# One order of the text for all engines, from the first load of x to the norm of k

## The chip, the cores and the metric

The kernel runs on one core of one Trainium2 chip. The metric is the device time of one execution in microseconds (us); lower is better. Times of the kernel before: 1184.32, 1184.76 and 1186.61 us in three runs, median 1184.76.

## What is computed

One layer of a hybrid decoder on x of 1024 positions by 1024 features in float32. Only the beginning matters here:

```
h = rmsnorm(x) * mix_norm
[q | k | v | u | s | gate_a | gate_b] = h @ w_in
q = rmsnorm(q per head) ; k = rmsnorm(k per head)      # 8 q heads, 2 kv heads of 64
```

After it come sliding-window attention, a spatial gating unit over chunks of 128 positions, a gated merge through three more products, and a gated MLP with a causal convolution of width 3. The output is (1, 1024, 1024) float32.

## The kernel before, in words

Every product is made in three matmuls: each operand is split into a high part, rounded to the matmul's float32r type, and a low part, the rest, and high·high, high·low and low·high are added up in PSUM (`mm3`, L91, the matmuls of L93, L94 and L95). A high part is a copy on ScalarE (`copy_hi`, L88 and L89), a low part a subtraction on VectorE or GpSimd. So each operand costs work on ACT, on DVE or POOL, and on PE.

The stage in question multiplies x with the k and v columns of w_in. The contraction of 1024 is cut into eight chunks k = 0 to 7. One array, xw, holds for each chunk the 128 rows of the norm's gain, of the k and v weights (256 columns) and of x (1024 positions), 1281 numbers a row, 640.5 KB a chunk. What follows happens per chunk, L227 to L254:

- `xload` (L203) brings the chunk from HBM over SP's queue (L206 and L207 for chunk 0, in two parts; L209 for the rest). Chunks 0 to 2 have the tile xf for themselves; chunks 3 to 7 share three buffers of the tag xr, so chunk 6 goes where chunk 3 was, and chunk 7 where chunk 4 was, and each waits until every reader of the old one is done. Five chunks are loaded ahead (L221); chunk k + 5 is asked for at the end of the pass for chunk k (L243).
- L229 copies the high part of the weights (wkv) on ACT, L230 makes the low part on DVE. L233 and L234 do the same with x, times the gain, in two halves of 512 positions (three pieces for chunk 0).
- L239 makes the 24 matmuls of the chunk, eight groups of positions by three, into the PSUM tiles pkv.
- `xsquare(k - 1)` (L211) squares the chunk before on ACT (L215 for chunk 0, L218 for the rest) and adds it to a running sum on DVE (L219).
- At k = 2 the text loads the two halves of the q weights (wq; L99 through `rload`), ident and cp (L247, L248); at k = 4 the first u weights (wu, L99), sink and ali (L251, L252).
- At k = 5 `rsplit` (L188) makes the high part of wq's first half on ACT and its low part on POOL (L193). After chunk 7 come the square of chunk 7, the second half of wq, and the split of the u weights: high on ACT, low on DVE (L256 to L259).

Then PE sums the squares over the partitions with ones as moving operand (tile ssq, L321), makes the first two q blocks (`q_proj`, L263), and the norm of k and the transposes follow, with the lines to L419 in an order written out by hand.

Two things set the order on an engine. Inside a `tc.manual_schedule()` the engines keep the order of the text; `build` (L35) holds one for PE over the whole kernel. Where an engine is in none, the framework's scheduler chooses from its own model of the times. Before the change, a manual order of all engines held from L317 to L420, and again from L1970 to the end. From L121 to L316, and from L421 to L1969, ACT, DVE, POOL and SP were in the scheduler's hands.

The body is long; the program prints the part that the diff touches.

Of the kernel before, what the change touches and what calls it, by code (L numbers as in the profile page):

```python
# [34 lines left out]
def build(tc, a):  # L35
    nc = tc.nc
    ctx = ExitStack()
    with ctx, tc.manual_schedule(engines={mybir.EngineType.PE}):
        body(ctx, tc, nc, a)


def body(ctx, tc, nc, a):
# [37 lines left out]
    def PH(s):  # L80
        if psum.get("H") is None:
            return PS(s)[:, 0:512]
        return psum["H"].tile([128, 512], F, tag="H", name=nm(s))
# [119 lines left out]
    def xload(k):  # L203
        xr[k] = x_first[:, k, :] if k < 3 else pa.tile([128, 1281], F, tag="xr", name=nm("xr"), bufs=3)
        if k == 0:
            nc.sync.dma_start(xr[k][:, 0:513], a["xw"][k, :, 0:513])  # L206
            nc.sync.dma_start(xr[k][:, 513:1281], a["xw"][k, :, 513:1281])  # L207
        else:
            nc.sync.dma_start(xr[k], a["xw"][k])  # L209

    def xsquare(k):  # L211
        for c in (L, H):
# [5 lines left out]
            nc.scalar.activation(sq, xs, AF.Square)  # L218
            nc.vector.tensor_tensor(sqsum[:, c], sqsum[:, c], sq, op=ALU.add)  # L219

    for k in range(X_AHEAD):  # L221
        xload(k)
    warm = PH("warm")
# [90 lines left out]
    kss3 = kss.rearrange("p (s g) -> p s g", g=2)  # L314
    krs3 = krs.rearrange("p (s g) -> p s g", g=2)

    man = tc.manual_schedule()  # L317
    man.__enter__()
    p_ssq = PH("ssq")
    for s in range(8):  # L320
        nc.tensor.matmul(p_ssq[:, 2 * s:2 * s + 2], sqsum[:, s * 128:(s + 1) * 128], ones,  # L321
# [323 lines left out]
    man = tc.manual_schedule()  # L645
# [1400 lines left out]
```

## Time and profile before

| | |
|---|---|
| time, median of three runs | 1184.76 us |
| time of the profiled execution | 1185.26 us |
| its span in the profile | 1183.5 us |
| granted TensorE clock over the span, mean | 0.998 |
| instructions | 15928 |
| matmuls recorded in the span | 5842 |
| PE idle in the first 31.41 us | 3.0 us |
| PE idle from 50 to 200 us | 3.1 us |

A row of the timeline has the start and the length in us, the engine, the line, the operation, output <- input with sizes and count, and in brackets how long the engine stood idle before it and what ended that. SPq is the queue on which SP issues transfers; the length there is that of the issue and not of the transfer. A row of the table of stretches has the stretch, its length, then for PE, PEld (weight loads), DVE, ACT and POOL the busy time and the number of instructions, then the granted clock, the share of the DMA engines and GB/s. In the view of DMA issues the last number is the time from issue to landing.

### The profile page before, as it was taken

Reading aid. Unit: us, or ns where it says so; the run is one execution under the profiler, and the core shown is the slowest. Engines: PE = TensorE matmul, PEld = TensorE weight load, DVE = VectorE, ACT = ScalarE, POOL = GpSimd, SP = SyncE. Lnnn points to the kernel's source line nnn. Section 1 sums busy time; section 2 is a strip of 40 time slices with the busy share of each in tenths; the row PEclk is TensorE's granted clock in tenths of the full one; section 3 lists DMA queues with packets and bytes.
Section 4 is the critical chain, followed back from the end, with each engine's and each line's share of the span. In section 5 each row is a group of like instructions: output and inputs, shape, how many; then the busy total and the mean of one; then the engine's idle time right before and its main releaser. Section 6 shows DMA issues by size and latency. Waiting matters only on the chain.

```text
span 1183.5 us, 15928 instructions
## 1 busy us (share of the span) xinstructions
PE 1170.3 (99%) x5842; PEld 990.4 (84%) x5842; DVE 874.5 (74%) x1037; ACT 566.5 (48%) x878; POOL 631.8 (53%) x435
## 2 busy tenths in 40 slices
PE   8999999999999999999999999999999999999998
PEld 8989989988888878888878888888888888888887
DVE  7798975743536776678788788877888797875674
ACT  8555667644336653335444443444444445425331
POOL 2467685488884764444867677776767541000000
PEclk9999999999999999999999999999999999999999
DMA  7110136157556654454545445455555268975471
GB/s 272 37 55 19 54 130 228 56 168 239 161 160 204 233 193 154 146 176 132 138 129 169 118 149 152 142 141 134 166 137 160 72 219 287 365 232 196 155 231 67
DMA packets 80942, 188.66 MB, mean 159 GB/s; under 512 B 9184, under 2 KB 16864, under 8 KB 80736
## 3 DMA queue, kind: packets, MB, share of 16 engines
q1 hardware_dynamic: 73008, 167.58, 40.7%
q0 software_dynamic: 7456, 15.73, 8.0%
q10 hardware_dynamic: 400, 4.33, 1.1%
q8 instruction: 46, 0.75, 0.3%
q14 instruction: 32, 0.26, 0.1%
HBM read 146.97 MB, written 49.02 MB: 166 GB/s over the span
## 4 chain that ended last, share of the span: by engine, by line
PE 82%; DVE 4%; POOL 3%; ACT 2%; issue 2%; DMA 1%; DVEq 0%; POOLq 0%; SPq 0%; ACTq 0%
PE pz L1060 50%; PE pd L1855 10%; PE pdy L1855 8%; PE px L95 2%; PE px L93 2%; PE px L94 2%; PE pu L95 1%; PE pu L93 1%; PE pu L94 1%; PE pv L517 1%; PE pq L93 1%; PE pq L95 1%; PE pq L94 1%; DVE xa L621 1%; DMA lq<-wup 0%
## 5 line engine op out<-in xcount | busy, mean ns | idle before, releaser
L1060 PE MATMUL pz<-T,qh 128*128 128x512 f32 x472 | 145.6, 390 | 0.0
L1060 PE MATMUL pz<-B,ph 128*128 128x512 f32 x352 | 109.7, 393 | 0.7 <-ACT x L1695 0.7
L1060 PEld LDWEIGHTS pz<-T,qh 128*128 128x128 f32 x472 | 88.4, 188 | 18.6 <-ACT u L885 0.3
L1019 POOL TENSOR_TENSOR pl<-lp,ph 128x1024 fp32r<-128x1024 f32 x30 | 73.2, 2439 | 52.9 <-ACT ph L89 52.9
L1060 PE MATMUL pz<-T,ql 128*128 128x512 f32 x236 | 91.8, 389 | 0.0
L1019 POOL TENSOR_TENSOR ql<-lq,qh 128x1024 fp32r<-128x1024 f32 x30 | 76.8, 2559 | 9.1 <-ACT qh L89 9.1
L1060 PEld LDWEIGHTS pz<-B,ph 128*128 128x128 f32 x352 | 65.1, 188 | 16.7 <-ACT x L1695 3.8
L1078 DVE TENSOR_TENSOR pz<-pz,rstd_b 128x1024 f32<-128x1024 f32 x60 | 73.9, 1232 | 4.6 <-ACT rstd_b L143 2.5
L1060 PE MATMUL pz<-T,s3h 128*128 128x512 f32 x232 | 71.4, 389 | 0.0
L1060 PE MATMUL pz<-y,wjh 128*128 128x512 f32 x224 | 69.5, 391 | 0.6 <-POOL y L1233 0.3
L1060 PE MATMUL pz<-B,pl 128*128 128x512 f32 x176 | 68.6, 390 | 0.0
L1855 PE MATMUL pd<-bh,ah 128*128 128x512 f32 x176 | 68.5, 389 | 0.0
L1855 PE MATMUL pd<-bl,ah 128*128 128x512 f32 x176 | 68.5, 389 | 0.0
L1855 PE MATMUL pd<-bh,al 128*128 128x512 f32 x176 | 68.5, 389 | 0.0
L1060 PE MATMUL pz<-T,AX 128*128 128x512 f32 x264 | 63.4, 389 | 0.0
L1060 PE MATMUL pz<-B,AX 128*128 128x512 f32 x264 | 63.4, 389 | 0.0
L1019 POOL TENSOR_TENSOR s3l<-lq,s3h 128x512 fp32r<-128x512 f32 x20 | 26.0, 1298 | 62.3 <-ACT s3h L89 62.3
L1060 PEld LDWEIGHTS pz<-T,AX 128*128 128x128 f32 x264 | 49.5, 188 | 10.3
L1060 PEld LDWEIGHTS pz<-B,AX 128*128 128x128 f32 x264 | 49.6, 188 | 10.3
L89 ACT ACTIVATE AX<-lr 128x1024 fp32r<-128x1024 f32 x22 | 23.4, 1063 | 70.9 <-POOL lr L621 70.9
L621 DVE TENSOR_TENSOR pz<-pz,u 128x512 f32<-128x512 f32 x37 | 25.9, 700 | 42.5 <-ACT u L1072 36.2
L1550 DVE SCALAR_TENSOR_TENSOR tg<-pz,cp,tg 128x1023 f32<-128x1023 f32 (+1 forms) x44 | 56.2, 1278 | 0.8
(359 smaller groups left out, 3597.6 us busy)
## 6 DMA issues: line engine op xcount, KB each, us to landing
lp<-wup SPq DMA_DIRECT2D x22, 512.0 KB, 3.8
lq<-wup SPq DMA_DIRECT2D x22, 512.0 KB, 4.2
ra<-wdown SPq DMA_DIRECT2D x44, 256.0 KB, 4.9
b<-T SPq DMA_DIRECT2D x44, 256.0 KB, 3.5
lq<-wup POOLq DMA_DIRECT2D x42, 256.0 KB, 5.3
B<-tv SPq DMA_DIRECT2D x33, 256.0 KB, 2.0
T<-tt SPq DMA_DIRECT2D x33, 256.0 KB, 2.1
b<-B SPq DMA_DIRECT2D x33, 256.0 KB, 3.0
```

The lines of the kernel that those rows point to most:

```text
L89: return nc.scalar.activation(dst, src, AF.Copy, scale=scale)
L93: nc.tensor.matmul(out, wh, mh, start=first, stop=False, **kw)
L94: nc.tensor.matmul(out, wh, ml, start=False, stop=False, **kw)
L95: nc.tensor.matmul(out, wl, mh, start=False, stop=last, **kw)
L517: nc.tensor.matmul(o, vhl[:, kb, g, :], w[:, 2 * g:2 * g + 2, :], start=i == 0 and g == 0, stop=i == len(ops) - 1, skip_group_check=True)
L621: eng.tensor_tensor(out, x, y, op=op)
L1019: nc.gpsimd.tensor_tensor(l, r, h.bitcast(F), op=ALU.subtract)
L1060: nc.tensor.matmul(o, p[:, k, :], m, start=not more and k == 0 and j == 0, stop=k == nk - 1 and j == 2, skip_group_check=True)
L1078: nc.vector.tensor_tensor(z, z, rstd_b, op=ALU.mult)
L1550: nc.vector.scalar_tensor_tensor(t[:, j:], p[:, 0:1024 - j], cw[:, ci, 2 - j:3 - j], t[:, j:], op0=ALU.mult, op1=ALU.add)
L1855: nc.tensor.matmul(o[d], p[:, k - k0, m], q[:, k - k0, :], start=new and k == 0 and j == 0, stop=k == HK - 1 and j == 2, skip_group_check= ...
```

## The change

The manual order of all engines, which began before the sums of squares (L317), begins before the first load of x (L221). No instruction is added or removed, no size changes, and PE had the order of the text in both.

```
@@ -218,6 +218,8 @@
             nc.scalar.activation(sq, xs, AF.Square)
             nc.vector.tensor_tensor(sqsum[:, c], sqsum[:, c], sq, op=ALU.add)
 
+    man = tc.manual_schedule()
+    man.__enter__()
     for k in range(X_AHEAD):
         xload(k)
     warm = PH("warm")
@@ -314,8 +316,6 @@
     kss3 = kss.rearrange("p (s g) -> p s g", g=2)
     krs3 = krs.rearrange("p (s g) -> p s g", g=2)
 
-    man = tc.manual_schedule()
-    man.__enter__()
     p_ssq = PH("ssq")
     for s in range(8):
```

In the text's order SP issues: chunk 0 in two parts, chunks 1, 2, 3, 4, 5, 6 and 7, the two halves of wq, ident, cp, wu, sink, ali. ACT takes for each chunk the weights' copy, the copies of x, and the squares of the chunk before; after those of chunk 4 the copy of wq's first half, then chunk 6.

More of the change, by code (lines that the diff above doesn't have):

```diff
@@ L219, in xsquare @@
             nc.vector.tensor_tensor(sqsum[:, c], sqsum[:, c], sq, op=ALU.add)
+    man = tc.manual_schedule()
+    man.__enter__()
     for k in range(X_AHEAD):
@@ L315, in body @@
     krs3 = krs.rearrange("p (s g) -> p s g", g=2)
-    man = tc.manual_schedule()
-    man.__enter__()
     p_ssq = PH("ssq")
```

## The prediction

> **What bounds the kernel now.** I read the page's shares first, then the chain that ended last, then a table of stretches, and only then, engine by engine in order of time, the stretch that the diff touches.
>
> ```profile
> PE 1170.3 (99%) x5842; PEld 990.4 (84%) x5842; DVE 874.5 (74%) x1037; ACT 566.5 (48%) x878; POOL 631.8 (53%) x435
> ...
> PE 82%; DVE 4%; POOL 3%; ACT 2%; issue 2%; DMA 1%; DVEq 0%; POOLq 0%; SPq 0%; ACTq 0%
> ```
>
> PE is busy for 99% of the span and holds 82% of the chain. So a microsecond by which PE falls behind early stays in the time, unless a later PE gap takes it up. The next rows (stretch, its length, then busy time and count of PE, PEld, DVE, ACT, POOL, then the granted clock) cut the edited stage out.
>
> ```profile
> 6.30:8.10 1.80, 1.75 (x8) 1.13 (x8) 0.95 (x3) 1.08 (x3) 0.00 (x0) 1.00 0.91 335
> 8.10:11.51 3.41, 3.41 (x16) 3.41 (x17) 2.95 (x6) 3.41 (x8) 0.00 (x0) 0.51 0.99 400
> 11.51:31.41 19.90, 19.90 (x171) 19.90 (x170) 19.90 (x32) 18.85 (x34) 4.88 (x2) 1.00 0.65 233
> 31.41:50.00 18.59, 17.62 (x151) 17.25 (x150) 11.24 (x30) 6.86 (x14) 6.90 (x5) 1.00 0.17 59
> 50.00:200.00 150.00, 146.90 (x1067) 135.93 (x1067) 121.29 (x251) 96.14 (x278) 101.53 (x107) 1.00 0.25 89
> ```
>
> PE multiplies k and v from about 6 to 31.4 us, after 8.10 without a gap. From 8.10 to 11.51 it runs at half clock (0.51). DVE is full as well and ACT nearly. Whoever delays the x copies on ACT by more than PE's small lead delays PE.
>
> ```profile
> 6.30 0.38 PE L93 MATMUL pkv<-wkv,x 128*128 128x256 f32 x1 [1.89 <-ACT x L89]
> ...
> 31.05 0.28 PE L93 MATMUL pkv<-wkv,x 128*128 128x256 f32 x1
> ...
> 31.41 1.84 PE L321 MATMUL ssq<-ones,rstd_b 128*128 128x2 f32 x16
> ```
>
> Three matmuls lie between 31.05 and 31.41, so one costs 0.12 us (I use 0.118), and a block of 24 (block k works on chunk k of the contraction, 0 to 7) costs 2.83. Counting two blocks back from 31.41, block 6 began at 25.75 and its third matmul, the first to need DVE's low part, was due at 26.0. That is the time to beat.
>
> **The change, part by part.** Nothing is computed that was not computed before; four queues get another order. PE had its text order already. SP is the queue that moves most.
>
> ```profile
> 0.81 0.38 SPq L209 DMA_DIRECT2D xr<-xw  x1
> 1.24 0.42 SPq L206 DMA_DIRECT2D xf<-xw  x1
> 1.72 0.43 SPq L207 DMA_DIRECT2D xf<-xw  x1
> 2.19 0.91 SPq L209 DMA_DIRECT2D xf<-xw  x2
> 3.15 0.93 SPq L209 DMA_DIRECT2D xr<-xw  x2
> 4.12 1.44 SPq L99 DMA_DIRECT2D wq<-wq  x2
> ...
> 18.13 0.33 SPq L209 DMA_DIRECT2D xr<-xw  x1
> 18.50 0.51 SPq L251 DMA_DIRECT2D sink_b<-sink  x1
> 20.70 0.33 SPq L209 DMA_DIRECT2D xr<-xw  x1
> 21.13 0.38 SPq L252 DMA_DIRECT2D ali<-ali  x1
> ```
>
> The scheduler issued one xr tile (x3) first, then both parts of x0, x1, x2, x4, x5; then it pulled both wq loads to 4.12, ahead of x6 (18.13) and x7 (20.70), which must wait for a free slot among the three xr buffers. In the text, x6 and x7 stand at k=1 and k=2, and wq, ident, cp, wu, sink and ali stand behind them. So SP will wait at x6 until x3's slot is free, at x7 until x4's, and wq leaves only after x7.
>
> *At the front, a gain.* Landing is issue plus the last figure of these rows, each from the view of DMA issues in a narrow window: x3 (issued 0.81), the first and second part of x0 (1.24, 1.72), x1 (2.19), x7 (20.70), ali (21.13).
>
> ```profile
> xr<-xw SPq DMA_DIRECT2D x1, 640.5 KB, 4.0
> xf<-xw SPq DMA_DIRECT2D x1, 256.5 KB, 4.2
> xf<-xw SPq DMA_DIRECT2D x1, 384.0 KB, 5.3
> xf<-xw SPq DMA_DIRECT2D x1, 640.5 KB, 6.8
> xr<-xw SPq DMA_DIRECT2D x1, 640.5 KB, 3.9
> ali<-ali SPq DMA_DIRECT2D x1, 512.0 KB, 4.8
> ```
>
> They landed at 4.8, 5.4, 7.0, 9.0, 24.6 and 25.9: after the first, about 1.6 to 2 us for each 640.5 KB. Without x3 ahead of it x0 starts some 1.6 us earlier (first part about 3.9) and x1 lands where the second full 640.5 KB landed, at 7.0. PE thus starts at about 4.7 instead of 6.30, and the half clock of 8.10 to 11.51, which follows PE's wait of 1.89, may be gone too. I count neither: block 6 will wait for ACT, whatever PE has gained before.
>
> *ACT's pace.* Block by block ACT makes one wkv copy, two x copies, two squares of the block before.
>
> ```profile
> 15.47 0.40 ACT L89 ACTIVATE wkv<-xr 128x256 fp32r<-128x256 f32 x1
> ...
> 18.04 0.40 ACT L89 ACTIVATE wkv<-xr 128x256 fp32r<-128x256 f32 x1
> 18.35 1.33 ACT L89 ACTIVATE x<-xr 128x512 fp32r<-128x512 f32 x2
> 19.58 1.09 ACT L218 ACTIVATE sq<-xr 128x512 f32<-128x512 f32 x2
> 20.62 1.05 ACT L89 ACTIVATE wq<-wq 128x1024 fp32r<-128x1024 f32 x1
> 21.57 1.09 ACT L218 ACTIVATE sq<-xr 128x512 f32<-128x512 f32 x2
> 22.61 0.40 ACT L89 ACTIVATE wkv<-xr 128x256 fp32r<-128x256 f32 x1
> ```
>
> From 15.47 to 18.04 is 2.57 per block. Blocks 1 to 5 from 7.0 end at 7.0 + 5 × 2.57 = 19.85, with the square of x4 last. That square frees x7's slot: before, it ended at 20.67 and SP issued x7 at 20.70. So x7 leaves at 19.85 (and x6, one block earlier, at 17.3, landing 21.2).
>
> *The added wait.* At k=5 the text puts the split of wq's first half behind that square. Before, wq had long landed and ACT took the copy at 20.62, while x6 was still on its way. Now wq stands right behind x7. The nearest row is ali, also 512 KB and also next behind x7: it landed 25.93 − 20.70 = 5.23 after x7's issue. So wq lands at 25.1 and ACT stands still for 5.2 us. Behind the copy on ACT lie block 6's wkv and x copies, then block 7's; DVE's low parts wait for them, and PE for both. Bounds: wq can come with x7 itself, 3.9 + 0.4 behind its issue (0.9 earlier), or share its time with the second wq half behind it (1.3 later, what 512 KB took between x7 and ali). The start of ACT's blocks can move by −0.6 (x0's copies done sooner than x1 is counted) to +0.8 (the square as late as before). I take the ali row, as the same size in the same place.
>
> Then: copy of wq until 25.1 + 0.95 = 26.05 (20.62 to 21.57), wkv 0.31, first x copy 0.71 to 27.1: PE begins block 6. DVE's low part takes 0.75:
>
> ```profile
> 14.83 0.75 DVE L234 SCALAR_TENSOR_TENSOR x<-xr,x 128x512 fp32r<-128x512 f32 x1
> ...
> 18.35 1.28 DVE L219 TENSOR_TENSOR rstd_b<-rstd_b,sq 128x512 f32<-128x512 f32 x2
> 19.55 0.42 DVE L230 TENSOR_TENSOR wkv<-xr,wkv 128x256 fp32r<-128x256 f32 x1
> ```
>
> So the third matmul runs at 27.85 instead of 26.0: **+1.85**. DVE needs about 2.86 per block (two sums 1.20, wkv 0.33, two low parts 1.33), so block 7's first low part is there at 27.85 + 2.86 = 30.7, when PE gets to it; nothing is added.
>
> *The clock behind the gap.* PE's blocks 1 to 5 follow x1: its first low part is ready at 7.0 + 0.31 + 0.71 + 0.75 = 8.75, and five blocks end at 22.7. From there to 27.1 PE stands 4.4 us. The trace has the half clock after a wait of 1.89; I expect it here as well. A stretch of 3.41 us holds 16 matmuls (the row of 8.10) instead of 3.41 / 0.118 = 29; 13 × 0.118 = **+1.5**. Bounds: 0, if the clock stays, and 3.0, if two stretches follow. The Trainium skill, "TensorE: Matmul & The Clock Gate", section "HAM oscillation — how this bites in real kernels", speaks against the change in the same place: PE gaps above some 3.4 us bring the half clock, at about 1.67 us each; by it the sum would be an estimated 3.5. The trace is stricter than that threshold, since 1.89 us went before a half-clock stretch here.
>
> *What is hidden.* ident, cp, wu, sink and ali now follow wq. From x7's landing (23.75) they and wq are some 2,200 KB, at 512 KB in 1.3 us about 5.6 us: all landed near 29.4, while their first readers after the squares, L259 for wu and L326 for sink, come after 32 (rows below). The second wq half: ACT reaches it after block 7 at 26.05 + 2 × 2.57 + 1.04 = 32.2, POOL's subtraction of 2.44 ends near 35.7, and PE wants it after ssq and half of the first q block, near 37.9. If that cover were gone PE would wait the difference.
>
> ```profile
> 21.75 2.44 POOL L193 TENSOR_TENSOR wq<-wq,wq 128x1024 fp32r<-128x1024 f32 x1 [18.05 <-ACT wq L89]
> ...
> 30.37 2.04 DVE L259 TENSOR_TENSOR u0l<-wu,u0h 128x1024 fp32r<-128x1024 f32 x1
> 32.33 0.16 DVE L326 TENSOR_SCALAR nsink<-sink_b 128x8 f32<-128x8 f32 x1
> ...
> 33.28 0.17 DVE L328 COPY ss<-ssq 128x8 f32<-128x8 f32 x1 [0.68 <-PE ssq L321]
> ```
>
> u0l starts after its high half (32.2 + 0.95 + 0.95 = 34.2) and ends at 36.2; PE's sums of squares end near 36.6. So the norm of k starts late by the same 3.4, no more.
>
> **Sum:** 1.85 + 1.5 = +3.4. On the profiled execution (1185.26, its span 1183.5 and 1.76 around it) that is 1188.7; on the median of the runs, 1184.76, it is 1188.2. I forecast **1188.4 us**.
>
> **The rivals.**
>
> *wq does not hold ACT* (the other side). If SP's queue keeps its old place for wq, or wq lands by 23.25 (25.1 − 1.85, that is 3.4 behind x7's issue), the front gain stays. x6 lands at 21.2: copies to 22.2, low part 22.95, block 6 to 22.95 + 22 × 0.118 = 25.55, block 7 on DVE's pace from 25.8, end 28.4 instead of 31.41: −3.0, 1182.2. For it: ACT and DVE have the pace. Against it: x7 alone took 3.9, and SP is among the engines ordered. It is also the case in which the change does not do on SP what it says. Chance 0.12.
>
> *The clock stays full* through the gap: +1.85, 1187.1. For it: the half clock follows a measure of activity whose place in time the trace shows once only. Against it: a gap more than twice that of 1.89. Chance 0.12.
>
> *The part behind the region comes out otherwise.* From line 420 to 1969 the scheduler still orders ACT, DVE, POOL and SP, and starts from another state. From 50 to 200 us PE is idle for 150 − 146.90 = 3.1: giving that back would bring 1185.6 (0.10); losing as much again, or two half-clock stretches, 1191.5 to 1193 (0.08). Against both: the loads it starts from (u, q) are wanted at 54 us and later.
>
> **How the numbers follow.** The forecast itself has 0.58, own range 1186.8 to 1190.9 (wq 0.9 earlier with the half clock short, to wq 1.3 later and 0.8 behind). The range takes in the clock staying and the give-back (0.58 + 0.12 + 0.10 = 0.80) and the bounds of wq's landing: 1184.8 to 1191.4. A difference under about 0.2% (2.4 us, edges 1182.4 and 1187.1) is no more than a measurement of this kernel can tell from none. Slower: 0.58, half of the clock case 0.06, the loss behind 0.08: 0.72. Same: 0.06 + 0.10 and a part of the fast case 0.03: 0.19. Faster: 0.09.
>
> **What would show it.** Right: x0 first on SP, x6 issued near 17.3, x7 near 19.9, wq right after it; an idle of about 5 us on ACT before wq<-wq, ended by its DMA; a PE gap of 4 to 5 us before a pkv matmul near 27, a granted clock of 0.5 behind it; ssq near 34.8; from then on rows like the old ones, 3.4 later. Wrong: wq issued before x6; ACT idle under 3 us there; ssq before 31.4; or ssq late while the end is not.

## The result

The changed kernel took 1193.14 us (median of three runs, 1192.68 to 1193.92) against 1184.76: a ratio of 1.0068, 95% interval 1.0045 to 1.009. It is slower, as forecast, but by 8.4 us and not by 3.6, and above the range's upper end of 1191.4. The profiled execution took 1192.68 with a span of 1191.0, 7.5 us longer than that of the kernel before; the account below is of these two executions.

The page of the profile after shows the same work: PE is still what bounds, with 5842 matmuls.

```profile
PE 1172.4 (98%) x5842; PEld 991.7 (83%) x5842; DVE 873.1 (73%) x1037; ACT 566.8 (48%) x878; POOL 631.8 (53%) x435
```

**SP's queue after** (timeline of the kernel after) has the order of the text.

```profile
0.81 0.39 SPq L206 DMA_DIRECT2D xf<-xw  x1
1.25 0.42 SPq L207 DMA_DIRECT2D xf<-xw  x1
1.72 0.90 SPq L209 DMA_DIRECT2D xf<-xw  x2
...
21.51 0.33 SPq L209 DMA_DIRECT2D xr<-xw  x1
21.89 0.90 SPq L99 DMA_DIRECT2D wq<-wq  x2
```

Chunk 0 is first. The row at 21.51 is chunk 7, which had to wait for chunk 4's slot. Only then do the two halves of wq leave, at 21.89, where they left at 4.12 before.

**ACT after** (its timeline; the bracket is the idle time before the row and what ended it):

```profile
20.39 1.09 ACT L218 ACTIVATE sq<-xr 128x512 f32<-128x512 f32 x2
27.65 1.06 ACT L89 ACTIVATE wq<-wq 128x1024 fp32r<-128x1024 f32 x1 [6.16 <-DMA wq<-wq]
28.61 0.40 ACT L89 ACTIVATE wkv<-xr 128x256 fp32r<-128x256 f32 x1
```

This is the predicted stall: the squares of chunk 4 end at 21.48, ACT stands for 6.16 us, and a transfer ends the wait. Block 6's copies stand behind it.

**DVE, POOL and PE after** (timeline, a few rows of the same stretch):

```profile
28.79 2.37 POOL L193 TENSOR_TENSOR wq<-wq,wq 128x1024 fp32r<-128x1024 f32 x1 [25.08 <-ACT wq L89]
29.04 2.40 DVE L232 TENSOR_TENSOR wkv<-xr,wkv 128x256 fp32r<-128x256 f32 x1 [5.68 <-ACT wkv L89]
29.68 0.58 PE L93 MATMUL pkv<-wkv,x 128*128 128x256 f32 x1 [3.98 <-ACT x L89]
31.49 0.58 PE L94 MATMUL pkv<-wkv,x 128*128 128x256 f32 x1 [1.24 <-DVE wkv L232]
32.16 0.58 PE L95 MATMUL pkv<-wkv,x 128*128 128x256 f32 x1
...
38.84 1.84 PE L321 MATMUL ssq<-ones,rstd_b 128*128 128x2 f32 x16
```

PE waits 3.98 us for the x copy and another 1.24 for DVE's low part. That low part took 2.40 us; in the kernel before, seven of the eight took 0.41 to 0.43. POOL's subtraction for wq, 28.79 to 31.16, lies beside it. The sums of squares, ssq, begin at 38.84, 7.43 later than the 31.41 of before. The span is 7.5 longer, so the loss is made here and nothing behind it gives any of it back.

**The clock** (table of stretches of the kernel after):

```profile
11.02:14.44 3.42, 3.42 (x19) 3.42 (x18) 3.02 (x6) 3.42 (x8) 0.00 (x0) 0.52 0.65 265
...
25.67:28.09 2.42, 0.02 (x1) 0.00 (x0) 0.00 (x0) 0.44 (x1) 0.00 (x0) 1.00 0.86 295
28.09:34.92 6.83, 3.93 (x15) 3.34 (x16) 5.88 (x8) 6.83 (x14) 2.37 (x1) 0.51 0.70 248
```

The first row is a half-clock stretch in block 1. After the stretch without PE, near 26, come 6.83 us, two times 3.41, at half clock, of which PE spends nearly half waiting anyway.

### The profile page after: what moved, and what is told of

The parts are those of the page before. It is cut to its first block, busy times and chain, and to the rows that moved or that the text cites. A ratio compares the mean times of both kernels' runs of the same rounds, so it can differ in the third digit from the quotient of the medians.

```text
span 1191.0 us, 15934 instructions
## 1 busy us (share of the span) xinstructions
PE 1172.4 (98%) x5842; PEld 991.7 (83%) x5842; DVE 873.1 (73%) x1037; ACT 566.8 (48%) x878; POOL 631.8 (53%) x435
## 4 chain that ended last, share of the span: by engine, by line
PE 81%; DVE 7%; POOL 2%; DMA 2%; issue 1%; ACT 1%; SPq 0%; DVEq 0%; ACTq 0%; POOLq 0%
PE pz L1060 52%; PE pdy L1855 8%; PE pd L1855 7%; PE px L95 2%; PE px L94 2%; PE px L93 2%; PE pu L95 1%; PE pu L93 1%; PE pu L94 1%; DMA wb<-wb 1%; PE pq L93 1%; DVE xa L621 1%; PE pq L95 1%; PE pq L94 1%; DVE ya L530 0%
## 5 line engine op out<-in xcount | busy, mean ns | idle before, releaser
L1550 DVE SCALAR_TENSOR_TENSOR tv<-pz,cp,tv 128x1023 f32<-128x1023 f32 (+1 forms) x44 | 56.2, 1278 | 0.8
```

The source lines that it names most:

```text
L1550: nc.vector.scalar_tensor_tensor(t[:, j:], p[:, 0:1024 - j], cw[:, ci, 2 - j:3 - j], t[:, j:], op0=ALU.mult, op1=ALU.add)
```

## The experiments

The theory ("Theory" in the expectations) is that of the prediction with what the trace added: wq leaves SP's queue behind chunk 7, ACT's copy of it stands in front of block 6, and then come the half clock and a DVE instruction held by POOL. Rival A says that the text's order on ACT, DVE and POOL costs the time by itself, whenever wq lands. Rival B says that it is the order in which the first x chunks are loaded. Each kernel's median stands beside that of the kernel before on the same chip.

### Whose order is it

**e1: SP back with the scheduler.** PE, ACT, DVE and POOL keep the order of the text, SP does not; before ssq the old region of all engines begins. Against the kernel before:

```
+    ET = mybir.EngineType
+    man = tc.manual_schedule(engines={ET.PE, ET.Activation, ET.DVE, ET.Pool})
+    man.__enter__()
     for k in range(X_AHEAD):
...
+    man.__exit__(None, None, None)
     man = tc.manual_schedule()
     man.__enter__()
```

> The manual order from the first load of x holds ACT, DVE, POOL and PE, and SP is left to the scheduler (from the sums of squares on all engines are manual again, as before). Theory (the loss is ACT waiting for wq at k=5, and it needs both orders together: SP's, which puts wq behind x7, and ACT's, which puts the copy of wq ahead of block 6): SP issues x3 first and wq before x6 again, ACT finds wq landed, ssq near 31.5, time 1184.5 to 1186. Rival A (the text order on ACT and DVE costs by itself: squares before the next copies, slots freed later): ssq at 34 or later, 1188 to 1192. Rival B (the order of the x loads costs, x0 first and x1 late): as the kernel before, so this run tells A from the rest.

Measured: 1186.58 against 1184.44, ratio 1.0016 (1.0007 to 1.0024), 0.6 us above the range expected. The timeline of e1:

```profile
21.96 1.05 ACT L89 ACTIVATE wq<-wq 128x1024 fp32r<-128x1024 f32 x1
...
23.91 1.89 DVE L233 TENSOR_TENSOR wkv<-xr,wkv 128x256 fp32r<-128x256 f32 x1
...
32.27 1.85 PE L325 MATMUL ssq<-ones,rstd_b 128*128 128x2 f32 x16
```

ACT's copy has no bracket: it waited for nothing. The loss at ssq is 0.86 us instead of 7.43. So with SP left to the scheduler the text's order on ACT, DVE and POOL costs about 2 us of the 8.4, and rival A does not explain the rest.

**e2: only SP (and PE) in the order of the text.** The same edit with `engines={ET.PE, ET.SP}`.

> The converse: SP and PE in the order of the text, ACT, DVE and POOL by the scheduler as far as the sums of squares. The program then has both halves of wq copied behind the squares of block 7. Theory (both orders are needed for the loss): x6 lands near 22.5 and x7 near 25.5, ACT goes on with them, PE reaches ssq at 30 to 31.5, the first q block waits up to 2 us for wq; time 1184 to 1187. Rival B (the order of the x loads costs by itself, x1 landing at 8.5 instead of near 7, slots freed late): ssq at 33 or later, 1187 to 1192. Rival A: as the kernel before, since ACT's order is the scheduler's.

Measured: 1184.62 against 1184.44, ratio 1.0001 (0.9992 to 1.001). wq still left behind chunk 7, at 20.94, but the scheduler put ACT's copies of it behind block 7. The timeline of e2:

```profile
27.90 4.79 POOL L193 TENSOR_TENSOR wq<-wq,wq 128x1024 fp32r<-128x1024 f32 x2 [24.20 <-DMA wq<-wq]
29.19 1.84 PE L325 MATMUL ssq<-ones,rstd_b 128*128 128x2 f32 x16
31.27 1.44 DVE L130 TENSOR_SCALAR rstd<-ss 128x8 f32<-128x8 f32 x1
38.30 0.66 PE L359 MATMUL pk<-ident,kr 128*128 128x128 f32 x4 [1.17 <-DVE kr L352]
```

The same products of k in the timeline of the kernel before:

```profile
38.85 0.60 PE L355 MATMUL pk<-ident,kr 128*128 128x128 f32 x4
```

ssq came 2.2 us earlier than before: SP's text order is a gain at the front, if ACT does not wait for wq. At the products of k only 0.55 of it is left. In between the late wq split sat on POOL beside the norm of k: a TENSOR_SCALAR on eight numbers a partition took 1.44 us (0.17 in the kernel before), and PE waited for the chain behind it. The profiled execution, at 1183.33 the fastest of this kernel's runs, still ends 1.9 us earlier than that of the kernel before, mainly since PE's wait of 0.7 us near 590 is missing in it; the medians are equal. So the loss needs both orders, SP's and ACT's.

**e3: all in the text's order, wq ahead of chunk 5.** The loads of wq, ident, cp and wu move to the pass of chunk 0.

```
-        if k + X_AHEAD < 8:
-            xload(k + X_AHEAD)
-        if k == 2:
+        if k == 0:
...
+            u_raw = [wload(a["wu"][0], "wu")]
+        if k + X_AHEAD < 8:
+            xload(k + X_AHEAD)
         if k == 4:
-            u_raw = [wload(a["wu"][0], "wu")]
```

> The changed kernel with the two halves of wq, ident, cp and the first u weights loaded at k=0, ahead of chunk 5 and so ahead of the two waits of SP; every engine in the order of the text. Theory: wq lands near 17, ACT finds it, the idle of 6.2 us before the copy goes; sq of block 4 ends near 21.5, wkv of block 6 near 22.8, its low part under POOL's subtraction to 25, ssq 31 to 31.8; time 1184 to 1186, 7 to 9 us under the changed kernel. Rival A and rival B: wq was not what ACT needed, x6 and x7 still leave at 18.9 and 21.5: ssq 34 or later, over 1188.

Measured: 1185.44 against 1184.44, ratio 1.0006 (0.9997 to 1.0015): nearly all of the loss is gone, with the order of the text on every engine. ssq is not where it was expected, though. The timeline and the stretches of e3:

```profile
22.00 1.05 ACT L89 ACTIVATE wq<-wq 128x1024 fp32r<-128x1024 f32 x1
...
23.47 2.36 DVE L232 TENSOR_TENSOR wkv<-xr,wkv 128x256 fp32r<-128x256 f32 x1
...
33.51 1.84 PE L321 MATMUL ssq<-ones,rstd_b 128*128 128x2 f32 x16
```

```profile
23.60:27.01 3.41, 1.89 (x14) 1.50 (x13) 3.41 (x3) 2.97 (x7) 1.94 (x1) 0.98 0.90 296
27.01:30.42 3.41, 3.41 (x18) 3.41 (x17) 3.41 (x7) 3.41 (x7) 0.00 (x0) 0.51 0.45 175
```

Here DVE's low part again took 2.36 us beside POOL, PE waited for it, and a stretch with 1.5 us of PE idle was followed by half clock in the next. ssq is 2.1 late. The profiled execution, at 1186.66, is the slowest but one of this kernel's runs, and the median is 1.2 lower; no trace shows where that comes from.

**e4: the split of wq's first half behind block 7.**

```
-        if k == 5:
-            rsplit(wq[0], rwq[0], 0)
...
+    rsplit(wq[0], rwq[0], 0)
```

> The changed kernel with the split of the first half of wq moved behind the square of block 7, ahead of that of the second half; SP keeps the order of the text, so wq still leaves behind x7. Theory: ACT goes from the square of block 4 (21.5) to block 6 as soon as x6 lands (22.7), block 7 at 25.4, no POOL work beside DVE's low parts of blocks 6 and 7; ssq near 30.3; POOL ends the two subtractions near 35, so the first q block waits 1 to 3 us; time 1184.5 to 1187. Rival A and rival B: ssq 33 or later, 1188 to 1192. If DVE held up by POOL was the larger part of the loss, this run and the one with wq ahead differ by 2 us in ssq.

Measured: 1187.69 against 1184.44, ratio 1.0027 (1.0017 to 1.0037), 0.7 us above the range expected. The timeline of e4:

```profile
23.63 0.43 DVE L232 TENSOR_TENSOR wkv<-xr,wkv 128x256 fp32r<-128x256 f32 x1
...
30.48 1.86 PE L320 MATMUL ssq<-ones,rstd_b 128*128 128x2 f32 x16
...
33.12 0.39 PE L94 MATMUL pq<-wq,x 128*128 128x256 f32 x1 [0.56 <-POOL wq L193]
36.48 0.58 PE L94 MATMUL pq<-wq,x 128*128 128x256 f32 x1 [1.50 <-POOL wq L193]
```

With no wait for wq ahead of block 6 and no POOL beside it, the low part is back at 0.43 and ssq begins 8.4 us earlier than in the kernel after. The wait has only moved: POOL's two subtractions now follow ssq, the q blocks wait 0.56 and 1.50 us for them, and a half-clock stretch lies from 34.60 to 41.40.

### The parts that the forecast had too small

**e5: without POOL's subtraction for wq's first half.** Those low parts are zero from the start, so this kernel leaves the low terms of that part of q out.

```
+    nc.gpsimd.memset(wq[0][:, 1, 0:4, :].bitcast(F), 0.0)
...
-            rsplit(wq[0], rwq[0], 0)
+            copy_hi(wq[0][:, 0, 0:4, :], rwq[0].rearrange("p (k a) b -> p k (a b)", a=2))
```

> The changed kernel without POOL's subtraction for the first half of wq: the low part of that half is set to zero near 4 us instead, so those low terms of q are left out. It tells what part of the loss was the low part of block 6's wkv taking 2.40 us on DVE beside POOL. Theory (DVE was held by POOL's instruction): that low part takes 0.42 us, PE's third matmul of block 6 runs near 30.2 instead of 32.16, ssq 36.7 to 37.9 instead of 38.84, 1 to 2 us under the changed kernel, 6 to 7.5 over the kernel before. Rival (the 2.40 us came from DVE's own wait for data or from the DMAs): 2.4 us again and the time of the changed kernel.

Measured: 1190.23 against 1185.16, ratio 1.0044 (1.0032 to 1.0057). The timeline of e5:

```profile
28.99 0.42 DVE L233 TENSOR_TENSOR wkv<-xr,wkv 128x256 fp32r<-128x256 f32 x1 [5.64 <-ACT wkv L89]
30.41 0.58 PE L95 MATMUL pkv<-wkv,x 128*128 128x256 f32 x1
37.84 1.84 PE L322 MATMUL ssq<-ones,rstd_b 128*128 128x2 f32 x16
```

The same instruction in the same place takes 0.42 instead of 2.40, and the third matmul of block 6 comes at 30.41 instead of 32.16, 1.75 earlier. That settles that POOL's subtraction held DVE. At ssq only 1.0 is left of it, since more of the matmuls now fall into the half clock (28.16 to 34.99). The span is 2.1 shorter. The other 1.1 lies far behind the stage, most of it near 1000 us, where PE waits 0.5 in the kernel after and not in e5; PE's waits there and near 590 us (0.3 to 0.9) come and go from trace to trace, so that about 1 us of a time is not explained by ssq.

**e6: chunk 0 in one transfer.**

```
-        if k == 0:
-            nc.sync.dma_start(xr[k][:, 0:513], a["xw"][k, :, 0:513])
-            nc.sync.dma_start(xr[k][:, 513:1281], a["xw"][k, :, 513:1281])
-        else:
-            nc.sync.dma_start(xr[k], a["xw"][k])
+        nc.sync.dma_start(xr[k], a["xw"][k])
```

> The changed kernel with chunk 0 loaded in one transfer of 640.5 KB instead of two. It asks why chunk 1 landed at 8.54 and not near 7.0. Theory 1 (the two parts with their short rows cost the DMA queue time): chunk 1 lands near 7 to 7.5, every later step 1 us earlier, 1 to 1.5 us under the changed kernel. Theory 2 (landing is set by something that all the first transfers share, 6.8 us after chunk 1's own issue as in both kernels): chunk 1 lands at 8 or later; PE starts later as it waits for all of chunk 0; ssq within 0.7 of 38.84 and the time of the changed kernel, since block 6 waits for wq either way.

Measured: 1190.70 against 1185.16, ratio 1.0047 (1.0032 to 1.0063). The same row of the DMA issues, chunk 1, first in the kernel after (issued at 1.72) and then in e6 (issued at 1.27):

```profile
xf<-xw SPq DMA_DIRECT2D x1, 640.5 KB, 6.8
```

```profile
xf<-xw SPq DMA_DIRECT2D x1, 640.5 KB, 5.2
```

Chunk 1 lands near 6.5 instead of 8.5. Only 0.45 of that is its earlier issue; with chunk 0 in two parts, 6.8 instead of 5.2 us pass from issue to landing. ACT's blocks move up and so does everything behind them (timeline of e6):

```profile
25.59 1.06 ACT L89 ACTIVATE wq<-wq 128x1024 fp32r<-128x1024 f32 x1 [6.07 <-DMA wq<-wq]
...
37.26 1.84 PE L317 MATMUL ssq<-ones,rstd_b 128*128 128x2 f32 x16
```

The wait for wq is as long as ever, 6.07, and ssq is 1.6 earlier than in the kernel after.

**e7: the scheduler's order of the first x loads.**

```
-    for k in range(X_AHEAD):
+    for k in (3, 0, 1, 2, 4):
```

> The changed kernel with chunk 3 loaded first, then 0, 1, 2 and 4, as the scheduler had it; all else in the order of the text, wq behind x7. Theory (the order of the x loads is not the loss; wq behind x7 is): chunk 1 lands at 9.0, the square of block 4 ends near 22, wq lands near 28, ssq 39 to 39.8, time 0.3 to 1 us over the changed kernel. Rival B (x0 first is the loss): ssq near 32, time within 2 us of the kernel before.

Measured: 1193.15 against 1185.16, ratio 1.0069 (1.0055 to 1.0083). The timeline of e7:

```profile
28.22 1.06 ACT L89 ACTIVATE wq<-wq 128x1024 fp32r<-128x1024 f32 x1 [6.14 <-DMA wq<-wq]
...
40.08 1.84 PE L321 MATMUL ssq<-ones,rstd_b 128*128 128x2 f32 x16
```

Giving SP's old beginning back does not help; ssq is even 1.2 later, though the time is that of the kernel after and not 0.3 to 1 us over it. Rival B falls.

**e9: 48 matmuls that nobody reads, in PE's gap.** They keep PE busy between block 5 and block 6, to separate the clock's part from the wait.

```
+        if k == 6:
+            fill = PH("fill")
+            for _ in range(48):
+                nc.tensor.matmul(fill[:, 0:256], hx(0, 5, slice(0, 128)), wkv[:, 0, 5, :], start=True, stop=True)
```

> The changed kernel with 48 extra matmuls of 256 columns on PE between block 5 and block 6, into a tile that nobody reads: they take PE's idle stretch (about 25.6 to 31.2) and nothing else. It tells the clock's part. Theory: the granted clock stays 1.00, block 6 from its third matmul (32.2) and block 7 run at 0.118 us a matmul, ssq near 37.6, 1.0 to 1.5 us under the changed kernel. Rival (the half clock cost nothing, since DVE's low parts set the pace of blocks 6 and 7): ssq 38.6 or later, no change in time.

Measured: 1194.95 against 1185.16, ratio 1.0087 (1.0073 to 1.0101). The clock stayed full and ssq came at 36.86, 2.0 earlier than in the kernel after (0.7 of it because ACT's copy of chunk 1 began at 7.81 instead of 8.54), but the time did not follow. The timeline of e9, 170 us later:

```profile
204.92 0.38 PE L93 MATMUL pvs<-wv,x 128*128 128x256 f32 x1 [1.26 <-DVE vg L764]
...
226.35 0.39 PE L93 MATMUL pm<-wgh,vsh 128*128 128x256 f32 x1 [1.53 <-ACT pm L930]
...
229.61 0.73 PE L1064 MATMUL pz<-x,ph 128*128 128x512 f32 x2 [1.62 <-DVE vg L764]
```

PE waits three times, 4.4 us in all, for PSUM tiles: twice until DVE has read an older one out, once until ACT has made its first write into a new one. In the kernel after only the wait for ACT is there, with 0.5. The one extra tile had moved every later tile one place on in a ring of four PSUM buffers, which are handed out in turn.

**e10: the same 48 matmuls in four tiles of 12,** so that the ring comes out where it was.

```
+        if k == 6:
+            for _ in range(4):
+                fill = PH("fill")
+                for _ in range(12):
+                    nc.tensor.matmul(fill[:, 0:256], hx(0, 5, slice(0, 128)), wkv[:, 0, 5, :], start=True, stop=True)
```

> The run with extra matmuls in PE's idle stretch once more, with the 48 matmuls in four PSUM tiles of 12 instead of one tile, so that every later tile of the ring of four gets the buffer that it has in the changed kernel. In the first try PE stood 2.0 us earlier at the sums of squares (0.75 of it since chunk 1 landed earlier) and lost 4.7 between 205 and 230 us, in three waits of 1.3 to 1.6 for a PSUM buffer. Theory (the shifted ring made that loss; the half clock costs 1.2): block 6 from its third matmul to the sums of squares takes 5.4 instead of 6.7, no new waits at 205 to 230, 0.8 to 2 us under the changed kernel, that is 6.3 to 7.7 over the kernel before. Rival (the extra matmuls themselves cost later, or an earlier PE runs into other waits): over the changed kernel again.

Measured: 1190.92 against 1185.21, ratio 1.005 (1.0036 to 1.0065); of the later waits only the 0.5 of the kernel after is there. The timeline and the stretches of e10:

```profile
31.95 0.39 PE L95 MATMUL pkv<-wkv,x 128*128 128x256 f32 x1 [0.27 <-DVE x L236]
...
37.51 1.84 PE L326 MATMUL ssq<-ones,rstd_b 128*128 128x2 f32 x16
```

```profile
28.09:34.92 6.83, 5.38 (x44) 4.92 (x43) 6.13 (x8) 6.83 (x14) 2.42 (x1) 1.00 0.72 241
```

In the very stretch that ran at 0.51 in the kernel after, the clock is 1.00. From the third matmul to ssq it is 5.56 us instead of 6.68 (38.84 − 32.16): the clock's part is 1.1.

### A version without the losses

**e11: chunk 0 whole, wq, ident, cp and wu ahead of chunk 6, the low part of u later.** All engines keep the order of the text. The edit is that of e6 and that of e3 with `k == 1` for `k == 0`, and DVE's low part of u moves behind the split of the second q block:

```
-    nc.vector.tensor_tensor(u_next[1], u_raw[0], u_next[0].bitcast(F), op=ALU.subtract)
...
+    nc.vector.tensor_tensor(u_next[1], u_raw[0], u_next[0].bitcast(F), op=ALU.subtract)
```

> A try at a version better than both: every engine in the order of the text, chunk 0 in one transfer, both halves of wq, ident, cp and the first u weights loaded ahead of chunk 6, and DVE's low part of the u weights moved behind the split of the second q block, where DVE had idle time. Worked out: chunk 1 lands near 6.5, the square of block 4 ends near 19.4, no wait for wq, the low part of block 6's wkv beside POOL until 23, ssq 29 to 30, the copy of the sums near 31.4 to 32.2 instead of 33.28 before; time 1 to 2.5 us under the kernel before. Rival (what is won ahead of the sums of squares is lost to the chain of the norm of k behind them, as in the run with SP alone in the order of the text): within 0.7 of the kernel before.

Measured: 1182.95 against 1185.21, ratio 0.9981 (0.9972 to 0.9989): faster than both kernels. The timeline of e11:

```profile
19.31 1.05 ACT L89 ACTIVATE wq<-wq 128x1024 fp32r<-128x1024 f32 x1
...
21.17 1.98 DVE L228 TENSOR_TENSOR wkv<-xr,wkv 128x256 fp32r<-128x256 f32 x1
...
29.35 1.84 PE L316 MATMUL ssq<-ones,rstd_b 128*128 128x2 f32 x16
31.23 0.17 DVE L323 COPY ss<-ssq 128x8 f32<-128x8 f32 x1 [0.48 <-PE ssq L316]
```

ssq begins 2.1 earlier than in the kernel before. From 9.45 to ssq the stage runs at full clock; up to there its matmuls are about 0.41 us long, as those of the kernel before are at half clock (8.42 to 11.5), though the table of stretches gives 1.00 for 3 to 31 us. DVE's low part is held here too (1.98), but PE still has matmuls of block 5 to do then, so no wait of PE follows from it: from 3 to 31 us PE is busy for 26.86 of 28.

**e12: the same without moving the low part of u.**

> The best version so far without the move of DVE's low part of the u weights: every engine in the order of the text, chunk 0 in one transfer, wq, ident, cp and wu ahead of chunk 6. Theory (the low part of u, 1.4 to 2 us on DVE, stands ahead of the chain of the norm of k): the sums of squares near 29.3 as with the move, their copy on DVE 0.5 to 1.5 us later than 31.2, time 0.3 to 1.5 us over the version with the move, 1 to 2 under the kernel before. Rival (the move did nothing): as the version with the move.

Measured: 1183.36 against 1184.83, ratio 0.9987 (0.9977 to 0.9996). ssq begins at 29.46, and the timeline of e12 has behind it:

```profile
29.68 1.95 DVE L257 TENSOR_TENSOR u0l<-wu,u0h 128x1024 fp32r<-128x1024 f32 x1
31.74 0.15 DVE L324 COPY ss<-ssq 128x8 f32<-128x8 f32 x1
```

The copy of ssq starts 0.5 later than in e11, behind u's low part. The two ratios' intervals overlap, so that the move pays by itself is seen in these rows but not in the times.

**e13: the kernel before, with chunk 0 in one transfer** (the edit of e6 on the kernel before).

> The kernel before, its order the scheduler's, with chunk 0 in one transfer and nothing else changed; chunk 3 still goes first. Theory (one transfer helps by letting chunk 1 land early, and only where chunk 0 goes first): chunk 0 lands at 6.4 to 7, PE starts 0.5 to 1 us later than 6.30, chunk 1 lands 1 to 2 us earlier than 9.0; PE is the bound of the stage, so ssq 31 to 32.5 and the time within 1 us of the kernel before. Rival (one transfer is all of what the best version wins): 2 us under the kernel before.

Measured: 1185.33 against 1184.83, ratio 1.0005 (0.9996 to 1.0014): no change. The whole chunk 0 alone is worth nothing where the scheduler orders the queue. What pays in e11 and e12 is the text's order together with wq ahead of chunk 6 and chunk 0 whole. e3, with chunk 0 in two parts and wq ahead of chunk 5, does not gain; which of the two differences matters there, no run separates.

## Why the direction was right and the size wrong

**Right** were the order on SP, chunk 7's wait for chunk 4's slot, wq directly behind it, ACT's wait in front of block 6 (6.16, forecast 5.2), that PE stands still behind it, the half clock, and that the rest follows as a block. e1, e2 and e3 each take one condition of that wait away, and 2.1, 0.2 and 1.0 us of the 8.4 are left. The size of PE's gap (3.98, forecast 4.4) is partly luck: PE ended block 5 at 25.70 instead of 22.7, since chunk 1 came 1.5 us later and the stretch from 11.02 to 14.44 ran at 0.52, and the x copy that ends the gap came at 29.68 instead of 27.1, so both ends were late. What was called hidden (ident, cp, wu, sink, ali, the second half of wq) cost nothing.

**The third matmul of block 6** was forecast at 27.85 and came at 32.16, 4.31 later. Three terms make that up.

1. *ACT's pace, step "x1 lands at 7.0".* Chunk 1's copy began at 8.54 and the squares of chunk 4 ended at 21.48 instead of 19.85: +1.63, where the prediction's bound was +0.8. The prediction took the landing from x1's place in the queue, as the second full 640.5 KB. It did not see that the two parts of chunk 0 hold it up: chunk 0 as one transfer brings chunk 1 to 6.5 (e6). Why two parts do that, no run shows.
2. *The added wait, "I take the ali row": 5.23.* From chunk 7's issue at 21.51 to the copy at 27.65 it was 6.14: +0.91, inside the bound of 1.3 given there. In e6 and e7, which also load wq behind chunk 7, ACT waits 6.07 and 6.14. Whether the second half behind it takes the time, no run shows; this stays open.
3. *"DVE's low part takes 0.75."* From the copy's start to the third matmul it was 32.16 − 27.65 = 4.51, forecast 27.85 − 25.1 = 2.75: +1.76. The prediction put the low part of the weights at nothing here, without a reason: it took the third matmul for the first that needs DVE, and counted the low part of x alone. The second matmul (L94) already needs the low part of the weights, which stands first on DVE, and beside POOL's subtraction that took 2.40 us instead of 0.42. In e5, without POOL, it takes 0.42, and from ACT's copy of wq (27.60) to the third matmul (30.41) it is 2.81, close to the forecast 2.75.

1.63 + 0.91 + 1.76 = 4.30, with a rounding of 0.01. The first and the third are the steps that failed: the one lies outside its bound, the other had none.

The third term could have been read ahead. The tile view of the kernel before groups the weight low parts as shortest, median and longest, in ns:

```profile
L230 DVE TENSOR_TENSOR wkv<-xr,wkv x5: 410/419/1424, 5.3 to 26.3; 128x256 fp32r<-128x256 f32 x5
```

One of five took 1424. In the timeline of the kernel before that one is block 6's:

```profile
22.40 0.68 DVE L219 TENSOR_TENSOR rstd_b<-rstd_b,sq 128x512 f32<-128x512 f32 x1
23.05 1.42 DVE L230 TENSOR_TENSOR wkv<-xr,wkv 128x256 fp32r<-128x256 f32 x1
```

It ends at 24.47, just behind POOL's subtraction of 21.75 to 24.19, while the sum L219 in front of it ran at its usual length. Before, PE's lead covered the 1 us. In the kernel after, ACT makes the wq copy and block 6's copy back to back, so POOL and DVE begin nearly together, and PE has no lead.

**The half clock** was forecast at +1.5. From the third matmul to ssq it is 6.68 against 5.41 before, +1.27, and e10 gives 1.1 for the clock alone. Two stretches came, not one, but PE had stood still in part of them. The 3.5 that the prediction worked out by the Trainium skill ("TensorE: Matmul & The Clock Gate", section "HAM oscillation — how this bites in real kernels") takes 1.67 us as lost time. The Trainium skill gives it as time at half clock, of which half is lost, so the estimate by it would be 2.7. The forecast did not use it.

**The sum** of what was measured at ssq: 1.85 forecast for the wait, 4.31 on top of it, and 1.27 for the clock give 7.43, the shift of ssq. The front gain that the prediction left out is real (−2.2 in e2, −2.1 in e11) but cannot be had while ACT waits. Of the rivals, "wq does not hold ACT" forecast ssq at 28.4 and 1182.2 us. e11 meets its condition and has 29.35 and 1182.95. e3 meets it too and has ssq at 33.51, since POOL held DVE there while PE had no lead, and half clock followed.

## What to carry to other kernels

An order written by hand applies to the queues as well: a load that stands behind one that waits for a buffer comes as late as that buffer, and a copy of it on an engine in order holds everything behind it, so the load should stand ahead of the first one that can wait. When work is moved together in time, look through the trace of before for the one instruction of a group that is much longer than its fellows, and ask what ran beside it. A filler or an extra tile in a rotating buffer is no neutral probe: count the ring.

## What the runs showed of the hardware

**DVE held by POOL.** With POOL's subtraction beside it, the weight low part (both inputs in SBUF) took 2.40, 2.36, 1.98 and 1.89 us (after, e3, e11, e1), without it 0.42 and 0.43 (e5, e4). No idle shows: the row is only longer, and in all four it ends 0.28 us behind POOL's row. The Trainium skill, "SBUF — State Buffer", section "Who interferes with whom", says that a DVE instruction with two inputs in SBUF contends with a GpSimd instruction that reads SBUF; the trace agrees. Short TENSOR_SCALARs on 128x8 numbers took 1.44 us in e2, 2.38 in e4 and 0.99 in e11 (0.16 or 0.17 in the kernel before), and each ended within 0.04 us of a POOL subtraction; that POOL held these too is argued from the rows, and no run takes POOL away there.

**The clock.** In e3 a half-clock stretch followed one in which PE had stood for 3.41 − 1.89 = 1.5 us, with no single long gap (1.24 and 0.28 were the waits in block 6). Together with the wait of 1.89 before, that is stricter than the threshold of the Trainium skill that the prediction cites. The waits alone do not decide it: in e10 waits of 1.18 and 0.27 in block 6 were followed by full clock, and in e4 half clock followed a stretch (31.18 to 34.60) in which PE stood for 0.56 us and for a third of the time worked at ssq's matmuls of two columns. What decides, no run shows.

**One extra PSUM tile** brought 4.4 us of waits 170 us later, where e10, with four, has 0.5.

**Chunk 0 in two parts** made the next transfer land 2 us later (after against e6). In the seven traces with the two parts first on the queue ACT's copy of chunk 1 begins between 7.81 and 8.90, in the three with one transfer first between 6.43 and 6.58. Behind chunk 3 the effect is not there: from chunk 1's issue to its landing it is 6.8 us in the kernel before and 6.7 in e13.
